# Local attention in three-stage steps: one block's scores, its predecessor's transposes, and the values' product of the block before that

## The chip, the cores and the metric

The kernel runs on one core of a Trainium2 chip. The metric is device microseconds of one execution. The engines of the core work in parallel, each through its own list of instructions in order: PE (matrix products, into the accumulator memory PSUM), DVE and ACT (element-wise work, both can read PSUM), POOL (element-wise work), SP (issues DMAs).

## The reference

One inference step of a two-layer decoder. The prompt has 16 meta tokens and 2048 tokens, model width 1024; eight decode samples of one token are carried along. Layer 0 feeds two head groups from one input projection: sliding-window attention (window 128, 8 query heads on 2 key/value heads of 64, a learned sink per head) and four gated delta-rule heads. Layer 1 is gated linear attention. Each layer has an output projection and a residual.

```python
def _sink_attend(q, k, v, mask, sink):
    s = jnp.einsum('...qhgd,...khd->...hgqk', q.astype(F32), k.astype(F32)) * (A_HEAD_DIM ** -0.5)
    s = jnp.where(mask[..., None, None, :, :], s, -jnp.inf)
    sk = sink.astype(F32)[:, :, None, None]
    m = jnp.maximum(jnp.max(s, axis=-1, keepdims=True), sk)
    p = jnp.exp(s - m)
    p = p / (jnp.sum(p, axis=-1, keepdims=True) + jnp.exp(sk - m))
    o = jnp.einsum('...hgqk,...khd->...qhgd', p, v.astype(F32))
    return o.astype(q.dtype)

# in _swa_prompt: blocks of 128 queries see their own and the preceding 128 keys
    mask = (diff >= 0) & (diff < WINDOW) & (kpos[:, None, :] >= 0)
    o = _sink_attend(qb, kband, vband, mask, sink)
# in _ab_layer
    oa = oa.reshape(Bn, T, A_WIDTH) * jax.nn.silu(za)
    mix = jnp.concatenate([oa, ob.reshape(Bn, T, B_VAL)], axis=-1)
    y = x + jnp.einsum('bte,ed->btd', mix, w_out)
```

## The kernel before

The prompt is worked through in four passes ("groups") of 512 tokens; the first also carries the meta tokens and the samples, so its projections have 536 columns in two halves of 268. Weights and activations of a projection are split in a high and a low part of a short float format, so a product of 128 input rows is three matmuls (high x high, high x low, low x high), and a projection with 8 input tiles is 24 matmuls of 512 columns into one PSUM bank (`proj`, tiles named `pp`, operands `t`, `wh`, `wl`).

The projections are the bulk work, run through `bulk`. Everything else is written as Python generators ("streams", started with `spawn`), each of which yields between its steps how long until its next step (in planned PE time) and how much PE time the step takes. `bulk` weaves a stream's step in when its time has come; the numbers are the table `DEF_LAT`, the planner's latencies. Streams of the same lane follow one another. `join` runs streams to their end where their results are needed. From the program in this order a scheduling layer then sets each engine's final order, moving instructions that its own estimate holds to be blocked; that final order is static, and the rows below show it.

In a pass the order of the attention layer is `ORDER`: heads c1, c2, c3 (`ab_conv`, three convolved projections and a gate, then the delta-rule stream `dn_head`) alternate with the pairs s0 to s3 (`ab_swa`: one query projection, one gate projection, then the stream `swa_pair`). A pair is one query head on each of the two key/value heads, and it goes through four blocks of 128 queries:

- `scores(b)` (S below): four PE matmuls of 256 columns (operand `kh`) into a `pc` bank, then on DVE mask and maximum (L991), a copy of the sink, a small step that makes the exponential's offset (L994, helper line L116), on ACT two exponentials with row sums (L996), on DVE a reciprocal (L997) and two scalings (L999, helper line L120).
- `values(b)` (V): four PE transposes (L1007) into a `pc` bank, and an ACT copy to SBUF (L1009).
- `out(b, PT)` (O): eight records of PE matmuls with the values (operand `va`) into a `pc` bank, and on DVE a multiply with the gate (L1018, helper line L113) into `z`.

After the fourth block `store_m` casts the whole `z` (512 columns) to the high part on ACT (L659) and subtracts on POOL for the low part; the output projection reads both. PSUM has eight banks: four for projections (`pp`), four for all streams (`pc`).

The output projection of the layer (`ab_out`) runs in two parts. The first uses three of the eight input tiles (two in the first pass). Then all heads and pairs are joined, and the second part adds the rest, for eight output tiles; its last input tile is pair s3's. The helper lines are L110 for every matmul, L113 for tensor-tensor, L116 for scalar-tensor-tensor, L120 for scaling.

Of the kernel before, what the change touches and what calls it, by code (L numbers as in the profile page):

```python
# [16 lines left out]
PSUM = bass.MemoryType.PSUM  # L17
# [11 lines left out]

ORDER = "c1 s0 c2 s1 c3 s2 s3".split()  # L30

DEF_LAT = dict(dn_spawn=3.0, dn_k=0.2, dn_q=0.6, dn_R=0.5, dn_kq=0.9, dn_kq2=3.6, dn_at=1.4, dn_i1=1.8, dn_ia=1.26, dn_ib=1.3, dn_m1=1.9, dn_m2=1.0, dn_v=2.0, dn_s1=1.4, dn_s2=1.4, dn_s3=1.2, dn_n=4.9, dn_o=1.5, sw_spawn=5.0, sw_0=4.2, sw_1=0.6, sw_2=1.96, sw_3=1.56, gl_spawn=2.8, gl_a=1.0, gl_t=3.3, gl_1=1.8, gl_2=3.5, gl_3=0.78, sd_1=5.0, sd_2=3.9, sd_3=3.64, dec_1=0.5, dec_2=4.0, rs=7.84, gm=2.0, gs_1=6.0, gs_2=4.55, rs0=1.3, sx_0=0.4, sx_1=3.25, sx_2=1.5, sx_3=5.0, sx_4=1.5, sx_5=3.0, fe_0=1.5, fe_1=1.0)

OUT_AB = (4, 5, 0, 1, 6, 2, 7, 3)
N_OUT0, N_OUT = 2, 3
# [34 lines left out]
def kernel(ctx: ExitStack, tc: tile.TileContext, ins, outs):  # L70
# [4 lines left out]
    wp = ctx.enter_context(tc.tile_pool(name="wp", bufs=2))  # L75
    dr = ctx.enter_context(tc.tile_pool(name="dr", bufs=2, space=bass.MemoryType.DRAM))
    wk = ctx.enter_context(tc.tile_pool(name="wk", bufs=2))
    pp = ctx.enter_context(tc.tile_pool(name="pp", bufs=4, space=PSUM))
    pc = ctx.enter_context(tc.tile_pool(name="pc", bufs=4, space=PSUM))

    cnt = [0]

# [8 lines left out]
    def ft(dt=F32, shape=(128, CMAX)):  # L91
        return wk.tile(list(shape), dt, tag="T", bufs=NT, name=nm("t"))
# [4 lines left out]
    def t512(shape=(128, 128), dt=F32):  # L97
        return wk.tile(list(shape), dt, tag="t512", bufs=4, name=nm("t5"))

    def sm(shape=(128, 32), dt=F32):  # L100
        return wk.tile(list(shape), dt, tag="sm", bufs=20, name=nm("sm"))

    def cb(shape=(128, 512)):
        return pc.tile(list(shape), F32, tag="pc", name=nm("pc"))
# [4 lines left out]
    def MM(out, lhsT, rhs, start=True, stop=True):  # L109
        T.matmul(out, lhsT, rhs, start=start, stop=stop)  # L110

    def TT(out, a, b, op, eng=None):
        (eng or V).tensor_tensor(out, a, b, op=op)  # L113

    def STT(out, a, s, b, op0, op1):
        V.scalar_tensor_tensor(out, a, s, b, op0=op0, op1=op1)  # L116

    def TS(out, a, s1, s2=None, op0=ALU.mult, op1=None):
        if op1 is None:
            V.tensor_scalar(out, a, s1, None, op0=op0)  # L120
        else:
            V.tensor_scalar(out, a, s1, s2, op0=op0, op1=op1)
# [247 lines left out]

    LAT = dict(DEF_LAT)
    LAT.update(outs.get("lat", {}))
# [68 lines left out]
    def give(tag, n=1):  # L441
        live[tag] -= n

    def until(cond):
        while not cond():
            yield 0.5, 0.0

    def take_in(tag, n=1):
        yield from until(lambda: room(tag, n))
        live[tag] += n  # L450
# [94 lines left out]
    def swa_extra(q, gx):  # L545
# [36 lines left out]
        for h in range(8):  # L582
            T.transpose(pt[0:16, 16 * h:16 * h + 16], S3[:, h, :], ident[0:16, 0:16])
        PT = t512((128, 128))[0:16]
        A.copy(PT, pt[0:16, 0:128])
        yield LAT["sx_2"], 0.3
        po = cb()
        for kv in range(2):
            MM(po[64 * kv:64 * kv + 64, 0:64], vm[0:16, 64 * kv:64 * kv + 64], PT[:, 64 * kv:64 * kv + 64])
        yield from until(lambda: gx)  # L590
# [24 lines left out]
        T.transpose(pt[:, 0:64], P, ident[0:64, 0:64])  # L615
        PT = t512((128, 64))
        A.copy(PT, pt[:, 0:64])
        yield LAT["sx_4"], 0.1
        po = cb()
        for b in range(8):  # L620
            MM(po[:, 8 * b:8 * b + 8], vc[b // 4][:, b % 4], PT[:, 8 * b:8 * b + 8])
        pos = t512((128, 64))
# [34 lines left out]
    def store_m(q, kt, z, c0, n):  # L657
        hi, lo = get_m(q, kt)
        A.copy(hi[:, c0:c0 + n], z)  # L659
        TT(lo[:, c0:c0 + n], z, hi[:, c0:c0 + n].bitcast(F32), sub, G)  # L660
# [288 lines left out]
    def ab_swa(q, u):  # L949
        g, off = q.g, q.off  # L950
        take("T", 3)
        QS = [ft(F32R, (128, 512)) for _ in range(2)]

        def ev_q(ps, c0, n):
            s = 0
            if g == 0:
                for kv in range(2):
                    A.activation(QX[:, 4 * kv + u, :], ps[64 * kv:64 * kv + 64, 0:EX], AF.Copy, scale=0.125)
                s = EX
            m = n - s  # L960
            for kv in range(2):
                r = slice(64 * kv, 64 * kv + 64)
                o = slice(64 - 64 * kv, 128 - 64 * kv)
                A.activation(QS[kv][r, 0:m], ps[r, s:n], AF.Copy, scale=0.125)
                STT(QS[kv][o, 0:m], ps[r, s:n], 0.125, QS[kv][r, 0:m].bitcast(F32), mul, sub)
        bulk(ab_proj(q, 1 + u, ev_q))
        gx = []
        if g == 0 and len(q.sw) == 3:
            q.xs = [spawn(swa_extra(q, gx), "sx", LAT["sx_0"])]
        Gt = ft()  # L970
        bulk(ab_proj(q, 5 + u, gate(q, Gt, u)))
        gx.append(1)
        return spawn(swa_pair(q, u, QS, Gt), "swa", LAT["sw_spawn"])

    def swa_pair(q, u, QS, Gt):
        g, off = q.g, q.off
        yield from take_in("T", 6)
        z = ft(shape=(128, 512))
        Sb = {}

        def scores(b):
            sc = cb((128, 2, 256))
            for kv in range(2):
                qq = QS[kv][:, 128 * b:128 * b + 128]
                MM(sc[:, kv], qq, KH[kv][0][:, 128 * b:128 * b + 256], stop=False)
                MM(sc[:, kv], qq, KH[kv][1][:, 128 * b:128 * b + 256], start=False)
            msk = CC[:, C_MSK0:C_MSK0 + 256] if (g == 0 and b == 0) else CC[:, C_MSK:C_MSK + 256]
            S_ = ft(shape=(128, 2, 257))
            st = sm((128, 8))
            for kv in range(2):  # L990
                V.tensor_tensor_reduce(out=S_[:, kv, 0:256], in0=sc[:, kv], in1=msk, scale=1.0, scalar=-3.0e38,  # L991
                                       op0=add, op1=amax, accum_out=st[:, kv:kv + 1])
            V.tensor_copy(S_[:, :, 256], RV[:, u:u + 5:4])
            STT(st[:, 2:4], st[:, 0:2], -1.0, nsink[:, u:u + 5:4], mul, amin)  # L994
            for kv in range(2):
                A.activation(S_[:, kv], S_[:, kv], AF.Exp, bias=st[:, 2 + kv:3 + kv], accum_out=st[:, 4 + kv:5 + kv])  # L996
            V.reciprocal(st[:, 6:8], st[:, 4:6])  # L997
            for kv in range(2):
                TS(S_[:, kv, 0:256], S_[:, kv, 0:256], st[:, 6 + kv:7 + kv])  # L999
            Sb[b] = S_  # L1000

        def values(b):
            S_ = Sb.pop(b)
            pt = cb((128, 2, 2, 128))
            for kv in range(2):
                for x in range(2):
                    T.transpose(pt[:, kv, x], S_[:, kv, 128 * x:128 * x + 128], ident)  # L1007
            PT = ft(shape=(128, 2, 2, 128))
            A.copy(PT, pt)  # L1009
            return PT  # L1010

        def out(b, PT):
            vp_ = q.vprev0 if b == 0 else q.vt[b - 1]
            po = cb()
            for x, vv in ((0, vp_), (1, q.vt[b])):
                for kv in range(2):
                    MM(po[64 * kv:64 * kv + 64, 0:128], vv[:, 64 * kv:64 * kv + 64], PT[:, kv, x], start=(x == 0), stop=(x == 1))
            TT(z[:, 128 * b:128 * b + 128], po[:, 0:128], Gt[:, off + 128 * b:off + 128 * b + 128], mul)  # L1018

        scores(0)  # L1020
        yield LAT["sw_0"], 0.45
        for b in range(4):
            if b < 3:
                scores(b + 1)
            if b == 2:
                give("T", 2)
            yield LAT["sw_1"], 0.45
            PT = values(b)
            yield LAT["sw_2"], 0.45
            out(b, PT)  # L1030
            yield LAT["sw_3"], 0.45
        store_m(q, u, z, off, 512)
        give("T", 5)
        yield 1.0, 0.0
# [923 lines left out]
```

## Time and profile before

| | |
|---|---|
| median of 3 runs | 2227.47 us (2224.37 to 2231.17) |
| profiled execution | 2228.4 us, span 2226.6 us, mean granted PE clock 0.987 |
| PE busy | 2151.5 us (97%), 17290 matmuls |
| DVE / ACT / POOL busy | 1230.4 / 836.2 / 265.7 us |
| chain that ended last | PE 70% of the span, 53% projections (`pp`), 14% other matmuls (`pc`, L110) |
| L991 mask and maximum, x128 | 50.4 us, 419 ns each |
| L996 exponentials, x128 | 64.1 us, 503 ns each |
| L1009 copy of the transposes, x64 | 37.4 us, 585 ns each |

A row of the timeline gives start and length in us, engine, line, operation, written tile <- read tiles, shape, how many instructions were merged in it, and in brackets the engine's idle time before it with the instruction that ended it. Lengths of matmuls are modelled with the drain, so consecutive ones overlap; the pace is the difference of starts. A waits row gives the total, the number and the longest. A stage row gives the stretch, its length, busy time and instructions of PE, weight load, DVE, ACT and POOL, then the granted PE clock, the share of the DMA engines and GB/s.

### The profile page before, as it was taken

How to read it: one execution, taken by the hardware profiler on the slowest of the kernel's cores; microseconds unless marked ns; L12 is line 12 of the kernel's file. 1: busy time of each engine (PE TensorE's matmuls, PEld its weight loads, DVE VectorE, ACT ScalarE, POOL GpSimd, SP SyncE). 2: the span in 40 equal slices, each digit the busy share in tenths (PEclk: the TensorE clock that was granted, in tenths of full speed). 3: DMA queues.
4: the chain of work that ended last, by engine and by line, in shares of the span. 5: the costliest groups of instructions: out<-in, count | busy, mean ns of one | idle time of the engine just before them, and what ended most of it. 6: DMA issues, size and time to landing. Idle time of an engine off the chain costs nothing.

```text
span 2226.6 us, 43788 instructions
## 1 busy us (share of the span) xinstructions
PE 2151.5 (97%) x17290; PEld 1808.8 (81%) x17290; DVE 1230.4 (55%) x3501; ACT 836.2 (38%) x2235; POOL 265.7 (12%) x314
## 2 busy tenths in 40 slices
PE   6999998999999999999999999999999999999997
PEld 6888888888879777788887777788887877778886
DVE  6678876655464566544345566545344466654323
ACT  4345544434352243333332244334333233334222
POOL 0011100011210011002220011002130000001111
PEclk8999999999999999999999999999999999999999
DMA  6563537758756723473555833364554743274444
GB/s 223 186 200 108 179 114 241 268 207 272 262 195 239 256 96 103 135 239 134 178 202 173 268 107 102 122 217 170 182 195 148 245 147 114 85 257 155 157 147 159
DMA packets 162623, 400.17 MB, mean 180 GB/s; under 512 B 22049, under 2 KB 54465, under 8 KB 162385
## 3 DMA queue, kind: packets, MB, share of 16 engines
q1 hardware_dynamic: 162416, 397.37, 52.5%
q8 instruction: 136, 2.23, 0.4%
q14 instruction: 71, 0.57, 0.1%
HBM read 297.19 MB, written 101.70 MB: 179 GB/s over the span
## 4 chain that ended last, share of the span: by engine, by line
PE 70%; DVE 4%; issue 2%; DMA 2%; ACT 1%; POOL 1%; SPq 0%; DVEq 0%; POOLq 0%; ACTq 0%
PE pp L110 53%; PE pc L110 14%; DVE t L116 1%; DVE t L113 1%; DVE inv L113 1%; PE pc L1007 1%; DMA t<-in_xT 1%; PE pc L1788 1%; POOL sm L206 1%; DVE t L120 0%; DVE t L991 0%; ACT t L996 0%; PE pc L1567 0%; PE pc L1442 0%; PE pc L1559 0%
## 5 line engine op out<-in xcount | busy, mean ns | idle before, releaser
L110 PE MATMUL pp<-t,wh 128*128 128x512 f32 (+1 forms) x4528 | 1264.7, 363 | 15.9 <-ACT t L150 7.6
L110 PEld LDWEIGHTS pp<-t,wh 128*128 128x128 f32 x4528 | 780.3, 190 | 126.9 <-issue 13.4
L110 PE MATMUL pp<-t,wl 128*128 128x512 f32 (+1 forms) x2264 | 808.2, 358 | 2.6 <-DVE wl L113 2.6
L110 PEld LDWEIGHTS pp<-t,wl 128*128 128x128 f32 x2264 | 428.8, 190 | 61.5 <-DVE wl L113 3.0
L113 POOL TENSOR_TENSOR t<-t,t 128x512 fp32r<-128x512 f32 (+3 forms) x128 | 164.3, 1301 | 521.4 <-ACT t L659 276.2
L110 PE MATMUL pp<-wh,t 128*128 128x256 f32 (+1 forms) x1088 | 208.8, 288 | 3.8 <-DVE QKt L113 3.8
L116 DVE SCALAR_TENSOR_TENSOR t<-t,PV,t 128x512 f32<-128x512 f32 (+4 forms) x232 | 176.1, 768 | 59.2 <-ACT t L1090 24.3
L110 PEld LDWEIGHTS pp<-wh,t 128*128 128x128 f32 x1088 | 172.1, 190 | 6.0 <-DVE QKt L113 4.0
L206 POOL TENSOR_TENSOR sm<-sm,mh 128x2 f32<-128x2 f32 (+3 forms) x84 | 68.5, 816 | 787.8 <-DVE sm L116 370.4
L116 DVE SCALAR_TENSOR_TENSOR t<-pp,t 128x512 f32<-128x512 f32 (+3 forms) x160 | 93.0, 586 | 122.1 <-PE pp L110 67.9
L110 PE MATMUL pp<-wl,t 128*128 128x256 f32 (+1 forms) x544 | 155.4, 286 | 0.0
L113 DVE TENSOR_TENSOR wl<-raw,wh 128x512 fp32r<-128x512 f32 (+3 forms) x138 | 91.3, 677 | 23.8 <-ACT wh L364 11.9
L110 PEld LDWEIGHTS pp<-wl,t 128*128 128x128 f32 x544 | 103.2, 190 | 0.6
L364 ACT CAST wh<-raw 128x512 fp32r<-128x512 f32 (+2 forms) x122 | 68.0, 587 | 53.2 <-DMA raw<-in_w_c 15.8
L113 DVE TENSOR_TENSOR t<-t,t 128x512 f32<-128x512 f32 (+4 forms) x103 | 62.9, 613 | 41.4 <-ACT t L488 40.1
L110 PEld LDWEIGHTS pc<-t,t 128*128 128x128 f32 (+4 forms) x496 | 63.7, 164 | 26.8 <-issue 6.5
L110 PE MATMUL pc<-t,t 128*128 128x128 f32 (+5 forms) x496 | 78.6, 269 | 6.5 <-DVE t L116 5.6
L113 DVE TENSOR_TENSOR QKt<-pp,t 128x512 f32<-128x512 f32 (+1 forms) x40 | 23.3, 586 | 110.9 <-PE pp L110 105.3
L996 ACT ACTIVATE t<-t,sm 128x257 f32<-128x257 f32 x128 | 64.1, 503 | 43.7 <-DVE sm L116 42.7
L488 ACT ACTIVATE t<-t 128x512 f32<-128x512 f32 (+1 forms) x70 | 44.1, 631 | 95.5 <-DVE t L116 68.7
L113 DVE TENSOR_TENSOR t<-pp,t 128x268 f32<-128x268 f32 (+1 forms) x90 | 44.5, 497 | 52.8 <-PE pp L110 35.5
L1009 ACT COPY t<-pc 128x512 f32<-128x512 f32 x64 | 37.4, 585 | 77.2 <-PE pc L1007 77.1
(334 smaller groups left out, 2810.8 us busy)
## 6 DMA issues: line engine op xcount, KB each, us to landing
wh<-wd SPq DMA_DIRECT2D x157, 512.0 KB, 3.7
wl<-wd SPq DMA_DIRECT2D x157, 512.0 KB, 4.8
wd<-wh SPq DMA_DIRECT2D x55, 512.0 KB, 4.2
wd<-wl SPq DMA_DIRECT2D x55, 512.0 KB, 4.2
t<-in_xT SPq DMA_DIRECT2D x72, 256.0 KB, 5.2
raw<-in_w_ab SPq DMA_DIRECT2D x25, 512.0 KB, 3.9
raw<-in_w_c SPq DMA_DIRECT2D x16, 512.0 KB, 5.6
out_yp<-t SPq DMA_DIRECT2D x32, 256.0 KB, 3.0
```

Source lines behind the costliest of these rows:

```text
L110: T.matmul(out, lhsT, rhs, start=start, stop=stop)
L113: (eng or V).tensor_tensor(out, a, b, op=op)
L116: V.scalar_tensor_tensor(out, a, s, b, op0=op0, op1=op1)
L206: G.tensor_tensor(out, x, mh[0:x.shape[0]].to_broadcast(list(x.shape)), op=ALU.pow)
L364: A.copy(hi[:, c], raw[:, c])
L488: A.activation(sq[:, :q.C], x, AF.Square)
L996: A.activation(S_[:, kv], S_[:, kv], AF.Exp, bias=st[:, 2 + kv:3 + kv], accum_out=st[:, 4 + kv:5 + kv])
L1007: T.transpose(pt[:, kv, x], S_[:, kv, 128 * x:128 * x + 128], ident)
L1009: A.copy(PT, pt)
L1788: T.transpose(oT[:, c], On[:, c, 128 * j:128 * j + 128], ident)
```

## The change

A step of a pair now does three things for three blocks, the oldest first: O of block i-2, V of block i-1, S of block i. There are six steps with one latency (4.5) between all of them, where there were thirteen with four latencies; the planned PE time of a step is the sum of its parts. The `pc` pool has five banks and the `pp` pool three.

```diff
-DEF_LAT = dict(..., sw_spawn=5.0, sw_0=4.2, sw_1=0.6, sw_2=1.96, sw_3=1.56, gl_spawn=2.8, ...)
+DEF_LAT = dict(..., sw_spawn=5.0, sw_p=4.5, gl_spawn=2.8, ...)
...
-    pp = ctx.enter_context(tc.tile_pool(name="pp", bufs=4, space=PSUM))
-    pc = ctx.enter_context(tc.tile_pool(name="pc", bufs=4, space=PSUM))
+    pp = ctx.enter_context(tc.tile_pool(name="pp", bufs=3, space=PSUM))
+    pc = ctx.enter_context(tc.tile_pool(name="pc", bufs=5, space=PSUM))
...
-        scores(0)
-        yield LAT["sw_0"], 0.45
-        for b in range(4):
-            if b < 3:
-                scores(b + 1)
-            if b == 2:
-                give("T", 2)
-            yield LAT["sw_1"], 0.45
-            PT = values(b)
-            yield LAT["sw_2"], 0.45
-            out(b, PT)
-            yield LAT["sw_3"], 0.45
+        PT = {}
+        for i in range(6):
+            if i >= 2:
+                out(i - 2, PT.pop(i - 2))
+            if 1 <= i <= 4:
+                PT[i - 1] = values(i - 1)
+            if i < 4:
+                scores(i)
+            if i == 3:
+                give("T", 2)
+            yield LAT["sw_p"], (1.35 if 2 <= i <= 3 else 0.9 if i in (1, 4) else 0.45)
         store_m(q, u, z, off, 512)
```

In the rows of the engines' orders, a row is line, operation, written tile <- read tiles, columns, and how many alike follow; `pp_11943` and the like are single PSUM tiles.

PE in the second pass, within pair s2, before: O of block 0, then S of block 2 and V of block 1, each between projection matmuls.

```order
L110 MATMUL pc_11576<-t_11556,va_538 64x128 x2
L110 MATMUL pc_11576<-t_11556,va_8328 64x128 x2
L110 MATMUL pp_11523<-t_8141,wh_11440 128x512
L110 MATMUL pp_11523<-t_8142,wh_11440 128x512
L110 MATMUL pp_11523<-t_8141,wl_11441 128x512
L110 MATMUL pc_11585<-kh_55_183,t_11266 128x256
L110 MATMUL pc_11585<-kh_56_184,t_11266 128x256
L110 MATMUL pc_11585<-kh_57_185,t_11267 128x256
L110 MATMUL pc_11585<-kh_58_186,t_11267 128x256
L110 MATMUL pp_11523<-t_8154,wh_11440 128x512
L110 MATMUL pp_11523<-t_8155,wh_11440 128x512
L110 MATMUL pp_11523<-t_8154,wl_11441 128x512
```

And the same place now: O of block 0, V of block 1 and S of block 2 in one piece, with a head's transposes (L1613) behind them.

```order
L110 MATMUL pc_11587<-t_11538,va_538 64x128 x2
L110 MATMUL pc_11587<-t_11538,va_8328 64x128 x2
L1007 MATMUL pc_11593<-CC_92,t_11545 128x128 x4
L110 MATMUL pc_11600<-kh_55_183,t_11246 128x256
L110 MATMUL pc_11600<-kh_56_184,t_11246 128x256
L110 MATMUL pc_11600<-kh_57_185,t_11247 128x256
L110 MATMUL pc_11600<-kh_58_186,t_11247 128x256
L1613 MATMUL pc_11616<-CC_92,t_11056 128x128 x4
L110 MATMUL pp_11641<-t_9491,wh_11514 128x512
```

V moved between O and S, and the projection's matmuls moved out from between the pieces.

PE at the end of pair s3 in the second pass, before: the second half of the last V, then the last O (`pc_11927`) and the second part of the output projection; `t_11933` is the high part that `store_m` makes.

```order
L1007 MATMUL pc_11920<-CC_92,t_11896 128x128 x2
L110 MATMUL pp_11971<-t_11074,wh_11939 128x512
L110 MATMUL pp_11971<-t_11075,wh_11939 128x512
L110 MATMUL pp_11971<-t_11074,wl_11940 128x512
L110 MATMUL pp_11971<-t_10963,wh_11939 128x512
L110 MATMUL pc_11927<-t_11925,va_8374 64x128 x2
L110 MATMUL pc_11927<-t_11925,va_8408 64x128 x2
L110 MATMUL pp_11971<-t_10964,wh_11939 128x512
L110 MATMUL pp_11971<-t_10963,wl_11940 128x512
L110 MATMUL pp_11971<-t_11741,wh_11939 128x512
L110 MATMUL pp_11971<-t_11742,wh_11939 128x512
L110 MATMUL pp_11971<-t_11741,wl_11940 128x512
```

The same place now, from the last projection matmuls ahead of the last V to the readers of the cast (`t_11934` is the low part).

```order
L110 MATMUL pp_12001<-t_11623,wh_11967 128x512
L110 MATMUL pp_12001<-t_11622,wl_11968 128x512
L1007 MATMUL pc_11920<-CC_92,t_11903 128x128 x4
L110 MATMUL pc_11927<-t_11925,va_8374 64x128 x2
L110 MATMUL pc_11927<-t_11925,va_8408 64x128 x2
L110 MATMUL pp_11943<-t_11933,wh_11801 128x512
L110 MATMUL pp_11971<-t_11933,wh_11939 128x512
L110 MATMUL pp_12001<-t_11933,wh_11967 128x512
L110 MATMUL pp_11943<-t_11934,wh_11801 128x512
L110 MATMUL pp_11943<-t_11933,wl_11802 128x512
L110 MATMUL pp_11971<-t_11934,wh_11939 128x512
```

The last O moved right behind the last V, and the first reader of the cast right behind O; three output tiles (`pp_11943`, `pp_11971`, `pp_12001`) stand open there, where there were two.

DVE at the same end, before: the masks of the last block (L991), the small step for its exponentials, then the multiply of the preceding block's O (`pc_11914`).

```order
L991 ISA t_11896,sm_11897<-pc_11891,CC_92 128x256
L991 ISA sm_11897 128x1
L116 SCALAR_TENSOR_TENSOR sm_11897<-sm_11897,nsink_158 128x2
L113 TENSOR_TENSOR t_11752<-pc_11914,t_11518 128x128
L997 RECIPROCAL sm_11897<-sm_11897 128x2
```

And now:

```order
L991 ISA t_11903,sm_11904<-pc_11898,CC_92 128x256
L991 ISA sm_11904 128x1
L113 TENSOR_TENSOR t_11809<-pc_11914,t_11513 128x128
L116 SCALAR_TENSOR_TENSOR sm_11904<-sm_11904,nsink_158 128x2
L997 RECIPROCAL sm_11904<-sm_11904 128x2
```

The multiply of the preceding O moved ahead of the small step.

More of the change, by code (lines that the diff above doesn't have):

```diff
@@ L30 @@
 ORDER = "c1 s0 c2 s1 c3 s2 s3".split()
-DEF_LAT = dict(dn_spawn=3.0, dn_k=0.2, dn_q=0.6, dn_R=0.5, dn_kq=0.9, dn_kq2=3.6, dn_at=1.4, dn_i1=1.8, dn_ia=1.26, dn_ib=1.3, dn_m1=1.9, dn_m2=1.0, dn_v=2.0, dn_s1=1.4, dn_s2=1.4, dn_s3=1.2, dn_n=4.9, dn_o=1.5, sw_spawn=5.0, sw_0=4.2, sw_1=0.6, sw_2=1.96, sw_3=1.56, gl_spawn=2.8, gl_a=1.0, gl_t=3.3, gl_1=1.8, gl_2=3.5, gl_3=0.78, sd_1=5.0, sd_2=3.9, sd_3=3.64, dec_1=0.5, dec_2=4.0, rs=7.84, gm=2.0, gs_1=6.0, gs_2=4.55, rs0=1.3, sx_0=0.4, sx_1=3.25, sx_2=1.5, sx_3=5.0, sx_4=1.5, sx_5=3.0, fe_0=1.5, fe_1=1.0)
+DEF_LAT = dict(dn_spawn=3.0, dn_k=0.2, dn_q=0.6, dn_R=0.5, dn_kq=0.9, dn_kq2=3.6, dn_at=1.4, dn_i1=1.8, dn_ia=1.26, dn_ib=1.3, dn_m1=1.9, dn_m2=1.0, dn_v=2.0, dn_s1=1.4, dn_s2=1.4, dn_s3=1.2, dn_n=4.9, dn_o=1.5, sw_spawn=5.0, sw_p=4.5, gl_spawn=2.8, gl_a=1.0, gl_t=3.3, gl_1=1.8, gl_2=3.5, gl_3=0.78, sd_1=5.0, sd_2=3.9, sd_3=3.64, dec_1=0.5, dec_2=4.0, rs=7.84, gm=2.0, gs_1=6.0, gs_2=4.55, rs0=1.3, sx_0=0.4, sx_1=3.25, sx_2=1.5, sx_3=5.0, sx_4=1.5, sx_5=3.0, fe_0=1.5, fe_1=1.0)
 OUT_AB = (4, 5, 0, 1, 6, 2, 7, 3)
```

## The prediction

> **What bounds the kernel now.** I read the head of the page first, then the busy time by stages, then who waits for whom on PE.
>
> ```profile
> span 2226.6 us, 43788 instructions
> PE 2151.5 (97%) x17290; PEld 1808.8 (81%) x17290; DVE 1230.4 (55%) x3501; ACT 836.2 (38%) x2235; POOL 265.7 (12%) x314
> ...
> 30.00:600.00 570.00, 533.30 (x5036) 481.88 (x5037) 392.22 (x1296) 254.03 (x713) 66.39 (x71) 0.97 0.59 199
> 600.00:1100.00 500.00, 494.63 (x3965) 409.13 (x3965) 269.74 (x729) 187.51 (x495) 57.43 (x72) 1.00 0.53 182
> ```
>
> PE is the bound: 97% busy, and 494.6 of 500 us in the second pass. Only the first pass (30 to 600 us) has idle time worth naming, 36.7 us. So a change can win only what PE waits or stumbles, and it loses whatever it adds there.
>
> ```profile
> PE pc L110 <- DVE inv L113: 7.8, 7, 2.0
> PE pc L1442 <- DVE CQ L116: 4.9, 7, 1.2
> PE pc L110 <- ACT t L1009: 2.1, 3, 0.7
> PE pp L110 <- POOL t L113: 1.5, 4, 0.5
> PE pc L1007 <- DVE t L120: 0.8, 2, 0.4
> ```
>
> The last three rows (total, times, longest) are the waits that local attention causes: 4.4 us in all of the program. No row names the release of a `pc` bank. So a fifth bank has no wait to remove; its own gain is put at nothing. The first two rows belong to the delta-rule heads that run beside it.
>
> **The change part by part.** No arithmetic is added or taken away; in passes 2 to 4 PE's order differs only within the attention layer, since after each of its ends 1570 rows stand as before (in the last pass the 1170 to the program's end). The step issues no DMA, and the cast and POOL's subtraction at the end of a pair are the old ones. What moves is where scores (S), transposes (V) and the values' product (O) stand among the projections' matmuls. Two things follow: PE is interrupted less often, and the end of the last pair gets less cover.
>
> **Interruptions.** Here is PE at the end of the attention in the second pass (start, length modelled with the drain; the pitch is the difference of starts).
>
> ```profile
> 937.77 0.40 PE L110 MATMUL pp<-t,wl 128*128 128x512 f32 x1
> 938.09 0.66 PE L110 MATMUL pc<-t,va 128*64 128x128 f32 x8
> 938.68 0.75 PE L110 MATMUL pc<-kh,t 128*128 128x256 f32 x4
> 939.27 0.63 PE L110 MATMUL pp<-t,wh 128*128 128x512 f32 x2
> 939.74 0.39 PE L110 MATMUL pp<-t,wl 128*128 128x512 f32 x1
> 940.21 0.68 PE L1007 MATMUL pc<-CC,t 128*128 128x128 f32 x4
> 940.64 0.71 PE L110 MATMUL pp<-t,wh 128*128 128x512 f32 x2
> 941.19 0.40 PE L110 MATMUL pp<-t,wl 128*128 128x512 f32 x1
> 941.42 0.39 PE L110 MATMUL pp<-t,wh 128*128 128x512 f32 x1
> 941.74 0.66 PE L110 MATMUL pc<-t,va 128*64 128x128 f32 x8
> 942.33 0.50 PE L110 MATMUL pp<-t,wh 128*128 128x512 f32 x1
> 942.66 0.40 PE L110 MATMUL pp<-t,wl 128*128 128x512 f32 x1
> ...
> 945.07 0.66 PE L110 MATMUL pc<-t,va 128*64 128x128 f32 x8
> ...
> 946.94 0.87 PE L110 MATMUL pp<-t,wh 128*128 128x512 f32 x3
> 948.13 0.50 PE L110 MATMUL pp<-t,wh 128*128 128x512 f32 x1 [0.33 <-POOL t L113]
> ```
>
> A projection's matmul takes 0.23 us (941.19 to 941.42). The one ahead of a lone O takes 0.32 and the one behind it 0.33: this stop costs 0.19 beside O's own 0.59. Behind V the pair of matmuls takes 0.55 in place of 0.47: 0.08. O with S right behind it (938.09) pays 0.09 at its entry and nothing at its exit. So a stop saved by setting two pieces side by side brings 0 to 0.19 us; I take 0.10, between the 0.08 and the 0.09. The two orders have 1408 and 1296 runs of projection or other matmuls on PE: 56 stops fewer, 26 of them in passes 2 to 4, 30 in the first. There I count half, as PE waits for weights and data anyway. Gain: 26 x 0.10 + 30 x 0.05 = 4.1 us (bounds 0 and 56 x 0.19 = 10.6).
>
> **The end of the last pair.** In the attention's last stretch (the output projection's second part) there is no other stream left; only open projection banks cover the chain. The other engines at the same place:
>
> ```profile
> 938.12 0.16 DVE L116 SCALAR_TENSOR_TENSOR sm<-sm,nsink 128x2 f32<-128x2 f32 x1
> 938.32 0.51 ACT L996 ACTIVATE t<-t,sm 128x257 f32<-128x257 f32 x1 [0.93 <-DVE sm L116]
> 939.45 0.17 DVE L997 RECIPROCAL sm<-sm 128x2 f32<-128x2 f32 x1 [0.55 <-ACT t L996]
> ...
> 945.77 0.29 DVE L113 TENSOR_TENSOR t<-pc,t 128x128 f32<-128x128 f32 x1 [2.31 <-PE pc L110]
> 946.10 0.62 ACT L659 CAST t<-t 128x512 fp32r<-128x512 f32 x1 [1.26 <-DVE t L113]
> 946.80 1.28 POOL L113 TENSOR_TENSOR t<-t,t 128x512 fp32r<-128x512 f32 x1 [20.02 <-ACT t L659]
> ```
>
> Before, the last S (938.68) and the last V were kept apart by eleven projection matmuls, V and O by four, O and the first reader of its cast by five. After, they are seven, none and none: with three `pp` banks, three output tiles are filled up to 12 of 15 matmuls and there is no fourth bank to start on. The four waits, for passes 2 to 4:
> - V, last block. DVE now has the multiply with the gate (of the preceding O) ahead of the small step that feeds the exponentials. From S's start: S 0.59, a matmul 0.23, entry 0.09, then O; O's start to the multiply 0.70 (945.07 to 945.77), multiply 0.2, small step to exponential 0.20, to the reciprocal 1.13 (938.32 to 939.45), to V 0.76 (940.21): 3.9 us; 3.7 if nothing stands between reciprocal and scaling. PE's own work up to there is 0.59 + 0.32 + 0.59 + 0.10 + 6 x 0.23 = 3.0. Wait 0.8.
> - O right behind V. The first pass shows this case:
>
> ```profile
> 355.69 0.60 PE L1007 MATMUL pc<-CC,t 128*128 128x128 f32 x4
> 357.02 0.66 PE L110 MATMUL pc<-t,va 128*64 128x128 f32 x8 [0.73 <-ACT t L1009]
> ```
>
>   1.33 us from V to O, of which V fills 0.4: lost 0.95 (the 0.73 leaves the modelled drain out).
> - The first matmul on the cast result: 945.07 to 946.10 plus 0.62 is 1.65 after O's start; O fills 0.59: 1.06.
> - The low part from POOL: 948.13 is 3.06 after O's start; 1.65 + 3 x 0.23 = 2.34 is filled: 0.72.
>
> Together 3.5 us. Before, the same place lost 0.5 (946.94 + 3 x 0.23 = 947.63, and the next came at 948.13). So +3.0 in each of three passes: +9.1. In the first pass a matmul covers half as much, so the end costs more (4.4 us, and a back-to-back V and O of 0.95 and smaller waits ahead of it), but before it waited there too: three times the ACT row's 0.7, once 0.4 for DVE and once 0.5 for POOL, 4.2 with the drains. I take +1.5.
>
> **The clock.** Waits that stand this close may bring the granted clock down:
>
> ```profile
> 815.30 0.45 PE L110 MATMUL pc<-inv,t 32*32 32x32 f32 x32 [1.16 <-DVE inv L113]
> 1786.64 0.45 PE L110 MATMUL pc<-inv,t 32*32 32x32 f32 x32 [1.97 <-DVE inv L113]
> 1787.02 1.22 PE L110 MATMUL pp<-t,wh 128*128 128x512 f32 x2
> ...
> 1780.00:1800.00 20.00, 18.03 (x323) 12.49 (x322) 13.09 (x37) 1.71 (x3) 0.00 (x0) 0.91 0.75 260
> ```
>
> After a wait of 1.97 us the matmuls ran at half pace, and the 20 us around it had a clock of 0.91: 1.8 us lost. The wait of 1.16 at 815 lies in the second pass, which the stages' row shows with a clock of 1.00. The new ends have no gap over 1.1 us but 3.5 us of them within about 6. I count one of the four as slowed: +1.8. [...]
>
> Sum: 9.1 + 1.5 - 4.1 + 1.8 = +8.3 us. The profiled execution took 2228.4 us (span 2226.6), 0.9 above the median of 2227.47; on the median's base that is 2235.8, so 2236.
>
> **The rivals.** A difference under 0.3%, 6.7 us, can hardly be told from no change here; so "same" is 2220.8 to 2234.2.
> - *The savings cancel the ends.* If every saved stop is worth a lone O's 0.19 (10.6 us) and no clock falls, the sum is 0: 2227.5. For it: O is the piece most often alone. Against: S and V cost 0.08 or less. Chance 0.35, all smaller sums included.
> - *Faster, by the heads' waits.* The steps' DVE work now comes in other places, and the rows for `inv` and `CQ` (7.8 and 4.9 us, 14 waits of the heads' first product and transposes; 15.5 us with 0.2 of drain each) could vanish. For it: in the new order the first `inv` product stands 14 or 15 matmuls behind the transposes it depends on, where it was 10 or 11. Against: a convolution step of DVE slips ahead of it, and the scaling for V now sits behind the same `CQ` step, so the wait turns into one of V. All of it gone gives 8.3 - 15.5 = -7.2, 2220.3; it decides only when more than nine tenths go. Chance 0.07.
> - *The clock falls at every end.* 3 x 1.8 more: 2241. For it: four gaps, close together. Against: a wait of 1.16 us alone left the clock at 1.00. Chance 0.15.
> - *My sum*, the ends outweigh the stops: chance 0.43.
>
> **How the numbers follow.** Slower is the sum and the clock's rival, 0.58; same 0.35; faster 0.07. The range runs from 2226 (savings near their upper bound, with a part of the heads' waits) to 2245 (all four ends slowed, and waits of V in the earlier blocks as well); it leaves out 0.2. The likeliest case alone is 2234 to 2240.
>
> **What the profile after would show.** Right: in passes 2 to 4, just ahead of the output projection's second part, PE rows with waits for the exponentials' scaling (L120), for ACT's copy of the transposes, for ACT's cast and for POOL, about 3 us a pass; ACT's row grows from 3 waits to at least 6. The span outside the attention stays within 1 us a pass. Wrong: if PE finds work there (its rows show no wait between the last V and the cast), if a lone stop turns out to cost nothing, or if the `inv` row shrinks by more than half.

## The result and the profile after

The changed kernel takes 2247.95 us, the median of 5 runs (2238.19 to 2249.94), against 2226.24 for the kernel before (5 runs, 2224.37 to 2231.17): ratio 1.0094 [1.0074, 1.0113], 21.7 us slower where 8.3 (2236) was forecast. The direction was right, the size was not, and 2247.95 lies above the range. The profiled execution took 2247.95 us.

The head of its page:

```profile
span 2246.1 us, 43774 instructions
PE 2161.0 (96%) x17290; PEld 1816.8 (81%) x17290; DVE 1218.3 (54%) x3501; ACT 837.2 (37%) x2235; POOL 263.7 (12%) x314
```

Its stages (start:end, length, busy time of PE, weight load, DVE, ACT, POOL, the granted PE clock, DMA share, GB/s):

```profile
300.00:375.00 75.00, 65.60 (x497) 58.47 (x496) 51.65 (x215) 30.91 (x97) 4.87 (x4) 0.91 0.49 152
375.00:600.00 225.00, 208.49 (x1502) 192.25 (x1502) 124.93 (x315) 94.28 (x205) 27.78 (x24) 0.96 0.68 234
600.00:1100.00 500.00, 494.52 (x3988) 409.30 (x3987) 264.95 (x723) 183.97 (x482) 60.74 (x72) 1.00 0.54 184
```

The same two first-pass stages of before:

```profile
300.00:375.00 75.00, 66.84 (x542) 60.55 (x541) 55.67 (x222) 32.55 (x96) 5.27 (x4) 0.98 0.53 171
375.00:600.00 225.00, 215.32 (x1561) 197.81 (x1560) 127.53 (x321) 94.21 (x206) 33.26 (x27) 0.97 0.73 250
```

In 300 to 375 us PE does 45 matmuls fewer, and the clock is 0.91 where it was 0.98; in 375 to 600 it does 59 fewer. The second pass's row is as full as before (494.5 of 500). So the first pass lost most. Exactly how much is seen by taking the start of one and the same ACT instruction in both kernels; the differences to the profiled execution of before, in us, for the changed kernel and for four of the experiments below, each by its profiled execution (left: time in before; 3+5 is three projection and five stream banks; the last pair's end of a pass, its first output tile, is at 366, 950, 1462 and 1977):

```
 before    changed  old steps,  new steps,  s3 in own   s3 in own lane,
   us      kernel   banks 3+5   banks 4+4   lane, 3+5   banks 4+4
  304.1     -0.6      -4.6        -1.7        +0.5        -3.1
  365.6     +7.5      -3.9        +4.5        -1.2        -1.7
  441.5     +8.4      -5.6        +1.2        +0.1        -1.8
  581.5    +15.6      -1.6        +3.5       +10.9        -4.4
  632.4    +15.8      -1.5        +3.7       +11.0        -4.3
  870.9    +11.8      -2.6        -1.0        +7.7        -8.5
  949.6    +20.3      -2.3        +7.2        +7.0        -9.3
 1060.1    +18.1      -2.4        +6.2        +9.2        -7.0
 1545.2    +19.0      -1.6        +8.9        +5.9       -12.5
 2059.9    +18.9      -4.9       +10.2        +0.4       -16.0
```

The changed kernel loses 15.8 of its 19.5 us of span in the first pass, 8 between 304 and 366 us and 7 between 441 and 581 (the pass's second layer). The later passes get 4 to 6 us ahead within the attention and fall 5 to 6 back by its end: 2.2, 0.9 and -0.1 on balance.

At those ends PE's rows are what the prediction said (end of the second pass; in brackets the wait):

```profile
962.70 0.40 PE L110 MATMUL pp<-t,wl 128*128 128x512 f32 x1
963.77 0.68 PE L1007 MATMUL pc<-CC,t 128*128 128x128 f32 x4 [0.68 <-DVE t L120]
965.12 0.66 PE L110 MATMUL pc<-t,va 128*64 128x128 f32 x8 [0.67 <-ACT t L1009]
966.82 0.97 PE L110 MATMUL pp<-t,wh 128*128 128x512 f32 x3 [1.04 <-ACT t L659]
968.18 0.60 PE L110 MATMUL pp<-t,wh 128*128 128x512 f32 x1 [0.39 <-POOL t L113]
968.58 0.63 PE L110 MATMUL pp<-t,wl 128*128 128x512 f32 x1
969.00 0.63 PE L110 MATMUL pp<-t,wh 128*128 128x512 f32 x1
...
971.56 0.53 PE L110 MATMUL pp<-t,wl 128*128 128x512 f32 x1
971.93 0.63 PE L110 MATMUL pp<-t,wh 128*128 128x512 f32 x2
972.39 0.39 PE L110 MATMUL pp<-t,wl 128*128 128x512 f32 x1
```

Four waits stand in a row. By the starts, less what each piece fills, they lose 0.84, 0.95, 1.11 and 0.67 us (962.93 to 963.77; 1.35 less 0.4; 1.70 less 0.59; 967.51 to 968.18), 3.6 in all; 0.8, 0.95, 1.06 and 0.72 were forecast. Behind them the pitch of a projection's matmul is 0.42 us (968.58 to 969.00) in place of 0.23, until about 971.6: the clock fell here too. It is 0.83 over 10 us at each of the three ends (965 to 975, 1480 to 1490, 1992 to 2002), a loss of 1.7 us of pace each. The list of waits groups them:

```profile
PE pc L110 <- DVE inv L113: 7.3, 9, 2.7
PE pc L1007 <- DVE t L120: 5.4, 9, 1.5
PE pp L110 <- ACT t L659: 4.2, 4, 1.0
PE pc L110 <- ACT t L1009: 3.4, 5, 0.7
PE pc L1442 <- DVE CQ L116: 1.4, 1, 1.4
```

### The profile page after: what moved, and what is told of

It reads as the page before. It is cut to its first block, busy times and chain, and to the rows that moved or that the text cites. A ratio compares the mean times of both kernels' runs of the same rounds, so it can differ in the third digit from the quotient of the medians.

```text
span 2246.1 us, 43774 instructions
## 1 busy us (share of the span) xinstructions
PE 2161.0 (96%) x17290; PEld 1816.8 (81%) x17290; DVE 1218.3 (54%) x3501; ACT 837.2 (37%) x2235; POOL 263.7 (12%) x314
## 4 chain that ended last, share of the span: by engine, by line
PE 70%; DVE 3%; ACT 2%; DMA 2%; issue 2%; POOL 1%; SPq 0%; DVEq 0%; POOLq 0%; ACTq 0%
PE pp L110 53%; PE pc L110 13%; DVE t L116 1%; PE pc L1007 1%; DVE t L113 1%; ACT t L996 1%; DMA t<-in_xT 1%; PE pc L1788 1%; POOL sm L206 0%; DMA t<-x2d 0%; POOL t L113 0%; DVE inv L113 0%; PE pc L1559 0%; DMA raw<-in_w_c 0%; DVE t L991 0%
## 5 line engine op out<-in xcount | busy, mean ns | idle before, releaser
L110 PEld LDWEIGHTS pp<-t,wh 128*128 128x128 f32 x4528 | 788.2, 192 | 136.0 <-issue 14.4
L991 DVE CUSTOM_DVE_ANT_0 t<-pc,CC 128x256 f32<-128x256 f32 x128 | 49.7, 422 | 24.4 <-PE pc L110 24.1
```

## The experiments

Every kernel was timed in 5 rounds against the kernel before on the same chip; differences below are the ratio, less one, times 2226, unless medians are named. An interval here is some 2.5 to 5.5 us to either side. Where only a part gets the old steps, the loop reads its steps from one of two tables with the old and the new latencies, for instance:

```diff
+        for w, lat, pe in (OLD if g == 0 else NEW):
+            for x in w.split():
+                ops[x[0]](int(x[1]))
+            yield LAT[lat], pe
+OLD = [("S0", "sw_0", 0.45), ("S1", "sw_1", 0.45), ("V0", "sw_2", 0.45), ("O0", "sw_3", 0.45), ...]
+NEW = [("S0", "sw_p", 0.45), ("V0 S1", "sw_p", 0.9), ("O0 V1 S2", "sw_p", 1.35), ...]
```

**Banks or steps, first pass or later ones.** The bank split alone (`pp` 3, `pc` 5 in the kernel before):

> The old thirteen steps of a pair, with three projection banks and five stream banks: the bank split alone. Theory S (the new steps cost the time: about 8 us in the first pass's attention, 8 us that follow from it in the first pass's second layer, 4 us in the later passes): within 2 us of the kernel before, 2224 to 2229. Theory B (the missing fourth projection bank costs the time: about 8 us in the first pass's second layer, where the order now has three open output tiles in place of four): 2232 to 2236, and the time from the end of the first pass's attention to the end of that pass grows by 8 us.

The steps alone (`pp` 4, `pc` 4 in the changed kernel):

> The new six steps, with four projection banks and four stream banks: the steps alone. Theory S: nearly the whole loss, 2240 to 2248. Theory B: the first pass's attention still loses up to 8 us, the second layer loses nothing, and the fourth bank covers the ends of the last pairs in the later passes: 2228 to 2235, and the waits for ACT's copy, for the cast and for POOL at those ends fall below 1.5 us a pass (they are 3.1 us in the changed kernel).

Old steps in the first pass (`OLD if g == 0`), and old steps in the later ones (`OLD if g > 0`):

> The changed kernel with the old steps in the first pass only (new steps in passes 2 to 4; three and five banks). Theory S: only the later passes' share stays, about 4 us: 2229 to 2233. Theory B: that share and the second layer's 8 us: 2236 to 2240. If neither holds and the loss is in the later passes after all, 2240 or more.

> The changed kernel with the old steps in passes 2 to 4 (new steps in the first pass only; three and five banks). Both theories: the first pass's 15 us stay, 2239 to 2244, some 4 us below the changed kernel; the ends of passes 2 to 4 show no wait for the cast. If the loss came from the ends of the later passes, 2228 to 2232.

Measured: the banks alone 2227.81, ratio 1.0011 [0.9997, 1.0024], +2.4 us, so theory B falls as the cause by itself; the steps alone 2238.77, 1.0062 [1.0044, 1.0081], +13.8, between the two theories. New steps in the later passes only: 2231.04, 1.0025 [1.0011, 1.0038], +5.6 with the banks' share; in the first pass only: 2241.38, 1.0067 [1.005, 1.0083], +14.9. The loss against the kernel before is mostly in the first pass, as the table above says, and it needs the steps; with the fourth projection bank back it is 7 to 9 us smaller (by the ratios, by the medians). The fourth bank did not cover the later ends, though. The steps alone have this there:

```profile
958.90 0.70 PE L110 MATMUL pp<-t,wh 128*128 128x512 f32 x2 [1.22 <-DMA wh<-wd]
962.18 0.80 PE L110 MATMUL pp<-t,wl 128*128 128x512 f32 x1 [2.58 <-DMA wl<-wd]
```

The waits for the copy and the cast are gone, and the weights are late instead. Four open output tiles hold eight weight tiles, a high and a low part each, and there are eight buffers; until the chain ends no further weight can be loaded.

**Which pair.** Old steps for s3 of passes 2 to 4 (`OLD if g > 0 and u == 3`), for s3 of the first pass (`OLD if g == 0 and u == 3`), and new steps only for s0 to s2 of passes 2 to 4, with four and four and with three and five banks (`OLD if g == 0 or u == 3`):

> The changed kernel with the old steps for the last pair (s3) of passes 2 to 4 only. Theory W (at each of these three ends 3.0 us of waits and one slow spell of the clock, 1.7 us, are real extra time, and what the later passes save in their attention is real too): the changed kernel's time less about 12 us, 2234 to 2238; PE shows no wait for the cast there and a clock of 1.00 at the three ends. Theory D (the attention only puts work off, and the ends pay it back; the later passes cost 1 us each on balance): only 2 to 4 us less, 2243 to 2247.

> The changed kernel with the old steps for the last pair (s3) of the first pass only, where the samples' stream runs beside it. Theory W (the waits between 325 and 375 us and the two slow spells there, 1.7 us each or double, are caused by the last pair's crowded end): 2239 to 2242, and the clock is 1.00 from 325 to 375 us but for one spell. Theory C (the loss of the first pass lies in the second layer, 440 to 600 us, whose order stays as in the changed kernel): 2246 to 2249.

> The new steps for pairs s0 to s2 of passes 2 to 4 alone; old steps in the first pass and for every s3; four and four banks. Theory W: the ends are covered and the savings of 3 to 4 us a pass remain: 2215 to 2221, faster than the kernel before. Theory D: nothing is saved, 2224 to 2229.

> As the run before, with three and five banks. Theory W: 2216 to 2223 (the bank split itself cost 2.5 us with the old steps). Theory D: 2226 to 2231.

Measured: 2238.81, ratio 1.0064 [1.004, 1.0089], below the changed kernel by 6.7 (by the ratios) or 9.1 us (by the medians); 2238.36, 1.0064 [1.004, 1.0087], below by 6.7 or 9.6; 2223.86, 0.9991 [0.9978, 1.0004]; 2225.43, 1.0005 [0.999, 1.002]. The first two are nearer to theory W than to its rivals: pair s3 carries most of the loss. The last two fit neither theory's range: the time shows nothing saved, although the ends are covered. But the savings may be there and hidden. In the run with four and four banks the heads' rows have already fallen (`inv` 7.8 to 3.2 us, `CQ` 4.9 to 0.4), and what stands at the ends now is again the weights:

```profile
PE pp L110 <- DMA wl<-wd: 5.4, 3, 2.1
```

**The waits and the clock by themselves.** Extra matmuls in the waits at the end of the last pair (`F3` is three of them, pinned to their place):

```diff
+       ("O1 V2 S3 G2", "sw_p", 1.35), ("O2 F3 V3", "sw_p", 0.9), ("F3 O3 F5", "sw_p", 0.45)]
```

> The changed kernel with 11 extra matmuls of 512 columns (0.23 us each, their results unused) at the end of the last pair in passes 2 to 4: 3 ahead of the last transposes, 3 ahead of the last values' product, 5 behind it. They fill PE's waits there and add work where they don't fit. Theory K (the slow spell of 1.7 us at each of the three ends comes from PE's idle time there): the clock is 1.00 at the three ends, and 3 x 1.7 us are saved less up to 0.5 us an end of extra work: 2242.5 to 2245. Theory N (the spells have another cause): they stay, 2247 to 2250.

> The same extra matmuls at the end of the last pair of all four passes. Theory K: the spell of the clock at the end of the first pass's attention (3.4 us between 365 and 375 us) goes too, and the one at 335 us, which belongs to the samples' stream, stays: 2239 to 2243. Theory N: 2247 to 2251.

Old steps for s3 in all passes (`OLD if u == 3`), and the kernel of the savings with nine weight buffers (and 50 activation buffers for 52):

> The changed kernel with the old steps for the last pair of all four passes. If the two parts found by the runs with the old last pair (9.6 us in the first pass, 9.1 us in the later ones) are separate: 2248.0 - 18.7 = 2229.3, 2227 to 2232. If they share a cause: 2234 to 2239.

> The run with new steps for s0 to s2 of passes 2 to 4 alone and four and four banks (2223.9 us), with nine weight buffers for eight, paid by 50 for 52 activation buffers. Theory L (at each end of passes 2 to 4 the open projection tiles hold all eight weight buffers, so that the next weight arrives late: three waits, 5.4 us in all): one more buffer lets the next weight's high part come early, the low part's wait shrinks to under 1 us each: 2219 to 2222. If the buffers aren't what holds the load back, or the activation buffers bind instead: 2223 to 2228.

With the waits filled in the later passes the clock stayed up. The stage at the second pass's end, changed kernel and then filled:

```profile
965.00:972.00 7.00, 5.45 (x21) 3.91 (x22) 2.26 (x4) 1.93 (x4) 1.28 (x1) 0.76 0.26 78
```

```profile
965.00:972.00 7.00, 6.64 (x34) 4.32 (x33) 2.70 (x6) 1.71 (x3) 1.28 (x1) 1.00 0.07 13
```

Behind it in the filled kernel PE waits 1.55 us for a weight (at 977.27), and its list of waits has a row that the changed kernel's has not:

```profile
PE pp L110 <- DMA wl<-wd: 4.1, 3, 1.6
```

Theory K is right on the cause of the spells (clock 1.00 for 0.76) but the time does not show what it expected of their cost: 2247.65, ratio 1.0095 [1.0075, 1.0114], no gain that these runs can tell. The issues of weight loads in the changed kernel at that place show why:

```profile
949.59 0.38 SPq L263 DMA_DIRECT2D wl<-wd  x1
968.81 0.32 SPq L263 DMA_DIRECT2D wh<-wd  x1
970.38 0.38 SPq L263 DMA_DIRECT2D wl<-wd  x1
```

For 19 us no load is issued. At full pace PE has used up the one weight loaded ahead before the next has landed, and waits 4.1 us at the three ends together; at half pace (0.42 us a matmul) it came later and waited for nothing. The slow spell had lain over the weight load. That takes most of the 5.1 us that the three spells were worth, not all of it: between 632 and 2060 us the filled kernel's profiled execution loses 0.8 us to before where the changed kernel's loses 3.1. It has a slow spell more in the first pass (clock 0.83 from 555 to 575 us, where the changed kernel has 1.00), with nothing changed there, and stands 3.4 us further back at 632; so the median may hide a small gain. Filling the first pass too gave 2245.28, 1.0088 [1.0071, 1.0105], 2.4 below the run before it by the medians, within the noise, and 2.3 above what theory K expected. Old steps for s3 everywhere: 2230.97, 1.0028 [1.0015, 1.0041], where 2229.3 was expected of separate parts; they add up. With nine weight buffers the 5.4 us above turned into this row, and the time is 2222.54, 0.9987 [0.9976, 0.9999], which the noise does not tell from the 0.9991 with eight. The edit did more than hold a ninth weight: with fewer activation buffers s3 also starts 7.3 us behind the last scores of s2 (926.75 to 934.08), where the run with eight has 14.8.

```profile
PE pp L110 <- DMA wh<-wd: 1.5, 3, 0.8
```

**Why s3.** None of this says why the last pair comes out so badly. The rows of the first scores do. The last scores of s2, the first of s3, and s3's last product in the first pass, before and then changed (the third line of before; in the changed kernel its transposes and the product behind them):

```profile
326.94 0.74 PE L110 MATMUL pc<-kh,t 128*128 128x256 f32 x4
336.78 0.72 PE L110 MATMUL pc<-kh,t 128*128 128x256 f32 x4
360.97 0.66 PE L110 MATMUL pc<-t,va 128*64 128x128 f32 x8
```

```profile
327.17 0.72 PE L110 MATMUL pc<-kh,t 128*128 128x256 f32 x4
346.65 0.63 PE L110 MATMUL pc<-kh,t 128*128 128x256 f32 x4
366.38 0.68 PE L1007 MATMUL pc<-CC,t 128*128 128x128 f32 x4 [1.45 <-DVE t L120]
367.74 0.48 PE L110 MATMUL pc<-t,va 128*64 128x128 f32 x2 [0.68 <-ACT t L1009]
```

The last scores of s2 stand at the same time (327), and s3 begins 9.8 us later before and 19.5 later now. Pairs share a lane, so s3 starts when the stream of s2 has ended. A stream was planned at 4.2 + 4 x (0.6 + 1.96 + 1.56) = 20.7 us; six steps of 4.5 are 27. Of the 27 us 13.5 follow the last scores, where 8.2 of the 20.7 did, 5.3 more. In the first pass slow PE adds to it (clock 0.66 from 335 to 345 us, where before it had 0.91). In passes 2 to 4 the same gap grows from 9.9 to 14.9 us:

```profile
916.65 0.64 PE L110 MATMUL pc<-kh,t 128*128 128x256 f32 x4
926.56 0.64 PE L110 MATMUL pc<-kh,t 128*128 128x256 f32 x4
```

```profile
932.45 0.72 PE L110 MATMUL pc<-kh,t 128*128 128x256 f32 x4
947.36 0.64 PE L110 MATMUL pc<-kh,t 128*128 128x256 f32 x4
```

The late start alone is not the whole of it. In the run with old steps for s3 of the first pass s3 starts just as late (its predecessor's last scores stand at 325.14), and yet the time is 7 to 10 us lower than the changed kernel's. Its last product comes 17.2 us after its first scores, where the changed kernel takes 21.1 (before, with the earlier start, 24.2).

```profile
344.65 0.63 PE L110 MATMUL pc<-kh,t 128*128 128x256 f32 x4
361.84 0.66 PE L110 MATMUL pc<-t,va 128*64 128x128 f32 x8
```

Between 304 and 366 us this run loses 3.4 us to before, the changed kernel 8.1. So it takes both: a late start, and six wide steps behind it. Two experiments change when s3 starts: the pace, so that a stream is planned at 20.7 us again, and the lane of s3.

```diff
-... sw_p=4.5, ...
+... sw_p=3.45, ...
```

> The changed kernel with the steps of a pair planned 3.45 us apart in place of 4.5, so that a pair's stream takes the 20.7 us it was planned at before. Theory Q (the last pair starts late, behind its predecessor in the lane, and ends late): the last values' product comes 4 us of PE work earlier in passes 2 to 4, the three later ends recover most of their 9 us, the first pass half of its 9.6 (its last product stays where it was): 2234 to 2239. Theory S (the crowded steps themselves cost it): the waits for the scaling (L120) grow instead, 2245 to 2250.

```diff
-        return spawn(swa_pair(q, u, QS, Gt), "swa", LAT["sw_spawn"])
+        return spawn(swa_pair(q, u, QS, Gt), "swb" if u == 3 else "swa", LAT["sw_spawn"])
```

> The changed kernel with pair s3 in a lane of its own, so that it need not wait for the end of s2; steps and banks as in the changed kernel. Theory Q: s3's first scores come 12 us of PE work earlier and its last product 3 to 7 us earlier; both the first pass's and the later passes' loss go: 2228 to 2234. Theory S: 2243 to 2249.

The same with four and four banks, and with nine weight buffers besides:

> The same with four and four banks. Theory Q: the bank split cost 9 us only where the end was late, so it matters little now: 2222 to 2229. Theory S: as the steps with four and four banks had it, 2236 to 2241.

> The same with four and four banks and nine weight buffers (50 activation buffers). Theory Q with the weight buffers: no wait for a late low part over 1 us at the ends: 2219 to 2225. Theory S: 2234 to 2240.

The lane settles it: 2223.59, ratio 0.9987 [0.9974, 1.0], 24 us below the changed kernel by one word, and below what theory Q expected. By the table only some 6 of them lie in the first pass (from 304 to 632 us it loses 10.5 us to before, the changed kernel 16.4); in passes 2 to 4 the changed kernel loses 3.1 us and this one gains 10.6. With four and four banks: 2213.56, 0.9949 [0.993, 0.9967], 11.4 us faster than the kernel before, below the expectation again; its reason, that the bank split costs only where the end is late, was wrong, as the split still costs 10 us here. Nine buffers on top (and 50 activation buffers), 2216.66, 0.9954 [0.9938, 0.997], add nothing: no row for late weights stands in the list of waits of either run. The pace was a miss: 2243.4, 1.0072 [1.0055, 1.0089]. In passes 2 to 4 it brought s3 closer (926.87 to 938.18, 11.3 us behind s2's last scores), and no wait for the cast is left at their ends. In the first pass s3 still starts 17.6 us behind (328.05 to 345.68), and by 632 us this run has lost 12.8 of the 14.9 us that it loses by 2060. The waits for the scaling (DVE `t` L120) grew in passes 2 to 4, from 2.7 to 4.5 us, too little to explain the rest.

So the pace did not test the first pass, and whether the new steps need their 4.5 us stays open; what they did not need was the queue behind them. With the own lane and four and four banks the end of the second pass has no wait ahead of POOL's. That place, and two rows of its waits:

```profile
935.78 0.66 PE L110 MATMUL pc<-t,va 128*64 128x128 f32 x8
936.37 0.73 PE L110 MATMUL pp<-t,wh 128*128 128x512 f32 x2
...
938.84 0.50 PE L110 MATMUL pp<-t,wh 128*128 128x512 f32 x1 [0.35 <-POOL t L113]
```

```profile
PE pc L110 <- DVE inv L113: 3.3, 6, 1.5
PE pc L1442 <- DVE CQ L116: 0.8, 1, 0.8
```

Eight matmuls of the projection stand between the last product and that wait, and the heads' rows fell from 7.8 and 4.9 us to 3.3 and 0.8. Last, the lane alone in the kernel before:

> The kernel before (old steps, four and four banks) with pair s3 in a lane of its own; its last values' product then comes 3.4 us of PE work earlier in passes 2 to 4. If the new steps are worth what the run with four and four banks showed: the old end cost only 0.5 us a pass and had cover, so 2222 to 2227 here, and the steps are worth some 10 us. If the lane alone makes the gain: 2212 to 2218.

2221.5, ratio 0.9987 [0.9976, 0.9998], 2.9 us. The remaining 8.5 us, give or take 5 by the two intervals, are the steps' own if the two add up.

## Why the prediction was wrong, point by point

- *The ends of passes 2 to 4*: right in place and size. In passes 2 and 4 the four waits that were named stand in a row, 3.6 us for 3.5 (second pass); in the third pass the slow spell had begun ahead of the wait for the low part, and only three are left. The ACT row for the cast has four waits, one for each pass, and a slow spell came in all three ends (clock 0.83 over 10 us each), which was the rival "the clock falls at every end". Most of its price did not count: the spell lay over a late weight, as the filled ends suggest (4.1 us of waits for weights came for 5.1 of spells).
- *The first pass, "I take +1.5"*: this is the step that failed. With the half stops against it (30 x 0.05) the first pass came to nothing in the sum; from 304 us on it lost 16.4 us. I compared the waits at the end, found that before had waited there too, and did not ask when the last pair would start. 8.1 of the 16.4 us fall between 304 and 366: s3 started 9.6 us later behind its predecessor, its six wide steps ended in waits (1.45 us for the scaling, 0.68 for the copy), and the clock of 300 to 375 us was 0.91 in place of 0.98, some 5 us. A lane of its own takes all of the 8.1 away, old steps for s3 more than half. The planner's table stood in the diff, and 20.7 against 27 us could have been added up. 7.2 more were lost in the second layer, which is the next point.
- *"A fifth bank has no wait to remove; its own gain is put at nothing"*: no run tells a gain of the fifth stream bank from the loss of the fourth projection bank, and that loss was costed only at the ends. Together they cost 2.4 us with the old steps (the interval reaches 0), and 7 to 10 with the new ones (2247.95 against 2238.77; 2223.59 against 2213.56). By the table this lies in the first pass's second layer, 441 to 581 us. Two waits of that stretch, before and then changed:

```profile
PE pp L110 <- DVE QKt L113: 3.8, 1, 3.8
PE pc L110 <- DVE Tg L116: 2.3, 2, 1.9
```

```profile
PE pp L110 <- DVE QKt L113: 5.6, 1, 5.6
PE pc L110 <- DVE Tg L116: 4.8, 2, 3.5
```

  They add up to 6.1 and 10.4 us. With three projection banks they are 8.3 with the old steps and 10.5 with the own lane, with four 5.9 with the new steps and 5.7 with the own lane. So they follow the bank split, and are 4.3 of the 7.2 us; what the rest is was not isolated. The profiled execution of the own lane with three and five banks (2230.0 us) lies above its median, so the 11 us of its column are too many.
- *Interruptions, 4.1 us saved (bounds 0 and 10.6)*: too small. Freed of the late start, the steps save some 8.5 us, in passes 2 to 4 by the table. The rows for `inv` and `CQ` lose 8.6 us between them, the mechanism of the rival "faster, by the heads' waits", to which I gave 0.07; with the lane alone and the old steps they stay (6.9 and 4.9 us). How much is left for the stops was not tested. In the changed kernel itself `CQ` fell from 4.9 to 1.4 and `inv` stayed (7.8 to 7.3).
- *The clock, "one of the four as slowed", 1.8 us*: too few. In the first pass alone four stretches of 10 us have a clock of 0.66 to 0.68, so about 3.4 us of pace lost in each (10 x 0.34), 13.4 us in all:

```profile
335.00:345.00 10.00, 9.70 (x58) 9.11 (x58) 5.66 (x26) 0.87 (x4) 0.00 (x0) 0.66 0.61 189
365.00:375.00 10.00, 6.58 (x33) 5.58 (x34) 4.57 (x12) 4.36 (x11) 1.27 (x1) 0.66 0.47 162
405.00:415.00 10.00, 8.74 (x48) 8.12 (x47) 4.32 (x9) 1.46 (x4) 1.59 (x1) 0.68 0.73 276
450.00:460.00 10.00, 5.76 (x26) 5.77 (x27) 6.43 (x21) 3.15 (x8) 5.56 (x4) 0.66 0.18 70
```

  Before, the stretches 335 to 345, 400 to 410 and 445 to 455 had 0.91, 0.83 and 0.83. By the stage rows of the result, 300 to 600 us lost 8.3 us to the clock before (75 x 0.02 + 225 x 0.03) and 15.8 now (75 x 0.09 + 225 x 0.04): some 7 us more. It is no accident of one execution: the mean granted clock was 0.980 to 0.983 in the five runs of the changed kernel, and 0.984 to 0.990 in the runs of the kernel before beside the experiments. Where the spells lie differs from profile to profile (335 to 345 us has 0.66 in the changed kernel and 0.83 in the run with all four ends filled), so how much of the first pass's loss is clock and how much waits is told by single profiles only.
- *"The span outside the attention stays within 1 us a pass"*: held in passes 2 to 4 (18.1 at 1060 us and 17.6 at 1184, for one), failed in the first by 7 us.

## What to carry to other kernels

When steps are merged or their latencies changed, add up the whole planned length of the stream first and look who waits in its lane: the last one of a lane sets the end of the stage. Cost such a shift in every stage by that stage's own cover, and against a run without it, not only against the kernel before: in the passes full of PE work the late start looked nearly free (3.1 us in the profiled execution), because it ate what the steps save there (10.6 us with a lane of its own). And cover is not free either: an open output tile holds its weight buffers, so the wait that more cover takes away can come back as a late load (1.22 and 2.58 us at the second pass's end, in the run of the steps alone).

## What the runs showed of the hardware

The clock fell after clusters of short waits. At the ends none was longer than 1.04 us, and three or four of them stood within about 5 us: 0.68, 0.67, 1.04 and 0.39 at the second pass's end, and in the third pass the clock was down behind 0.68, 0.68 and 1.04. Filled with matmuls, these ends kept a clock of 1.00 (965 to 975, 1480 to 1490 and 1992 to 2002 us, where the changed kernel has 0.83). In the stretches shown a spell lost about 1.7 us of pace or twice that: from 968 to 972 us the clock of each microsecond was 0.72, 0.50, 0.50 and 0.57, about 3.4 us at half pace, and from 337 to 344 it was 0.50 in six of them and 0.60 in the seventh, about 6.8. And such a spell did not cost in full where something else was late: at the later ends, taking away three spells (5.1 us) brought 4.1 us of waits for weights.
